# A planner's assumed DMA rate, lowered from 295 to 280 for the last token group of a decoder block

## The chip, the cores and the metric

The kernel runs on one core of one Trainium2 chip, as one program. The metric is the device time of that program in microseconds (us); of several runs the median counts. Engines are called by the profile's names: PE is TensorE, PEld its weight loads, DVE is VectorE, ACT is ScalarE, POOL is GpSimd and SP is SyncE.

## What is computed

One layer of a decoder block on 1024 tokens with 1024 channels, all in float32. Three token mixers (stick-breaking attention, dilated window attention, attention into 256 memory tokens) run on one normalised input, are gated and summed, and go through an output projection. Then comes an expert layer, which is what the change is about:

```python
s1, i1 = lax.top_k(sc[:, :, 0], 16); s2, i2 = lax.top_k(sc[:, :, 1], 16)
...
top_s, pos = lax.top_k(cand, PEER_TOPK)
idx = jnp.take_along_axis(cand_idx, pos, axis=-1)
gate = jax.nn.softmax(top_s, axis=-1)
...
act = gelu(einsum('chkd,cd->chk', u[ic], hc)); w = gc * act
return einsum('chk,chkd->cd', w, v[ic])
```

Each token has 8 heads, and each head picks 16 of 16384 experts. An expert is a row of 1024 numbers in a table `u` and one in a table `v`. A token's 128 chosen rows of `u` are multiplied with the token, and the 128 rows of `v` are summed with the weights that come out.

## The kernel before, in words

The 1024 tokens are 8 tiles of 128. They go through the mixers in three groups, `GROUPS = (2, 3, 3)`: group 0 holds tiles 0 and 1, group 1 tiles 2 to 4, group 2 tiles 5 to 7. `phase1` (one call for each group) runs these stages in order: stick-breaking, dilated and memory attention, gating (weights `w_gate` and `w_o`), the output projection (`out_proj`, weights `w_out`), the norm (`ffn_norm`) and the experts' query projection and choice (`select`, weights `w_pq`; the rest of the choice is `topk`, run in small pieces beside other work by `sides`).

The expert layer is done in two ways. Tiles 4 and 6 (`DENSE`) are done densely: all 16384 experts are multiplied, in the generator `dense`, which begins when the last group has ended and `stored` holds both tiles. The six other tiles are done by gathers (`Experts`). A gather step (`Experts.step`) handles one choice for each of 128 rows: POOL issues an indirect DMA of 128 rows of `u` and one of 128 rows of `v` (L1097, 0.5 MB each), DVE multiplies the `u` rows with the tokens' rows `hb` and sums (L1151), ACT and DVE make a weight, and PE adds the weighted `v` rows into `po` (L1177). PE and ACT also spread the tokens' rows into `hb` (L1090, L128). A tile has 128 steps, so there are 768 steps in all. `u` blocks are fetched 5 steps ahead, `v` blocks have 6 buffers (`UP, VP = 5, 6`).

A tile can be gathered once `topk` has put its row numbers, `iT`, and its weights, `gT`, (L1011 and L1013) into the list `ready`. Tiles 0 and 1 become ready when group 0 ends and are gathered while group 1 is computed; tiles 2 and 3 beside group 2; tiles 5 and 7 beside the dense part.

What is issued between two gather steps is set by a planner at the end of `block_kernel`. It keeps two running sums, `pe` and `dma`, in planned ns. A piece of the main work (`fill`, one `yield` of `rest()`, which chains the three groups and `dense`) adds its matmul cost times `slow` to `pe`, and its bytes divided by the rate `bw[0]` to `dma`. A gather step adds `TOKEN_NS` = 700 to `pe`, and `TOKEN_BYTES / bw[0]` to `dma`:

```python
            while filler[0] is not None and (dma > pe or pe < due):
                a, b = fill(1)
                pe += a
                dma += b
            pe += TOKEN_NS
            dma += TOKEN_BYTES / bw[0]
            if ex.step():
```

So a smaller rate makes a gather step look longer, and more main work is issued between two steps. The rate is `BW[0]` = 295 (bytes per ns) for the three groups, and `rest()` sets it to `BW[1]` = 360 when the groups are over (L1405). `TOKEN_BYTES` is 1,073,152, so that a step counts 3638 ns at 295. When the main work is used up, the remaining steps are issued one after the other. The planner's sums only set an order; they are not times of the chip. A scheduler then puts each engine's queue in order.

Of the kernel before, what the change touches and what calls it, by code (L numbers as in the profile page):

```python
# [34 lines left out]
RUN = 22  # L35


BW = 295.0, 360.0
SLOW = 1.38, 1.1
TOKEN_NS, TOKEN_BYTES = 700.0, 128 * 8192 + 3 * 8192.0  # L40
LEAST = 3000.0
# [36 lines left out]
def block_kernel(ctx: ExitStack, tc: tile.TileContext, io):  # L78
# [109 lines left out]
    def gap_tables():  # L188
        d32 = tmp.tile([128, 32], F32, name="on")
        nc.vector.tensor_scalar(d32, iota[:, :32], 4.0, rows[:, 1:2], op0=OP.mult, op1=OP.subtract)  # L190
        for (dil, nb), o, w, num in zip(DIL, gofs, gwid, gnum):
            diff = dmat if dil == 1 else d32
            for bd in range(num):
                c = o + (num - 1 - bd) * w
                t = gaps[:, c:c + w]
                bad = tmp.tile([128, 128], F32, name="on")[:, :w]
                b2 = tmp.tile([128, 128], F32, name="onm")[:, :w]
                nc.vector.tensor_scalar(t, diff, -1.0, 128.0 * bd, op0=OP.mult, op1=OP.add)
                nc.vector.tensor_scalar(bad, t, 0.0, HUGE, op0=OP.is_lt, op1=OP.mult)
                nc.vector.tensor_scalar(b2, t, float(128 * dil), HUGE, op0=OP.is_gt, op1=OP.mult)  # L200
                nc.vector.tensor_max(bad, bad, b2)
                if dil > 4:
                    gi = small.tile([128, 32], I32, name="gi")
                    nc.vector.tensor_copy(gi, t)
                    nc.vector.tensor_scalar(gi, gi, dil - 1, None, op0=OP.bitwise_and)
                    nc.vector.tensor_scalar(b2, gi, 0.0, HUGE, op0=OP.not_equal, op1=OP.mult)
                    nc.vector.tensor_max(bad, bad, b2)
                nc.vector.tensor_max(t, t, bad)
# [36 lines left out]
    def load(out, src):  # L245
        count(out)
        nc.sync.dma_start(out, src)
# [81 lines left out]
    def norm_T(xT, n, gain, out):  # L329

        p = bank()
        for k in range(KD):
            sq = tmp.tile([128, NMAX], F32, name="sq")
            actf(sq[:, :n], xT[:, k, :n], AF.Square)
            mm(p[:, :n], ones, sq[:, :n], start=k == 0, stop=k == KD - 1)
        yield
        y = rstd_rows(p[:, :n], n, D)
        for k in range(KD):
            nc.vector.scalar_tensor_tensor(out[:, k, :n], xT[:, k, :n], gain[:, k:k + 1], y[:, :n],
                                           op0=OP.mult, op1=OP.mult)  # L340
        yield
# [23 lines left out]
    def both(gidx, h, n):  # L365

        if gidx not in SPLIT:
            return h, None
        parts = []
        for k in range(0, KD, 4):  # L370
            parts.append(tuple(x.rearrange("p (k n) -> p k n", k=4) for x in spare()))
            halves(*(x[:, :, :n] for x in parts[-1]), (h[0] if type(h) is list else h)[:, k:k + 4, :n])
        return h, parts
# [21 lines left out]
    def memory_kv(pipe, weights, mh):  # L395
        kv = big.tile([128, 2048], F32, name="big")
        kTm = kv[:, :1024].rearrange("p (h m) -> p h m", h=4)
        vm = kv[:, 1024:].rearrange("p (m c) -> p m c", m=2)
        for h in range(4):
            p = proj_T(weights("w_kv", h), mh, MEM)  # L400

            def done(y, p=p, h=h):
                nc.vector.scalar_tensor_tensor(kTm[:, h, :], p[:, :MEM], gk_mem, y[:, :MEM],
                                               op0=OP.mult, op1=OP.mult)
            part = head_norm(p, MEM, 128, ones, done)
            pipe.tick()
            pipe.push(part)
            yield
        for h in range(4):
            proj_v(weights("w_kv", 4 + h), mh, 2, vm[:, :, h * 128:(h + 1) * 128], 0)  # L410
            pipe.tick()
            yield
        nc.scalar.dma_start(c_mem, kv)

    def subs(G):

        return [(i, min(SUB, G - i)) for i in range(0, G, SUB)]

    def stick_breaking(pipe, weights, hT, n0, G, oT):
        N = G * 128  # L420
        t0 = n0 * 128
        for p in range(4):
            kv = big.tile([128, 2048], F32, name="big")
            kT = kv[:, :1024]
            v = kv[:, 1024:].rearrange("p (t c) -> p t c", t=NT)
            if n0:
                load(kT[:, :t0], c_sbk[p, :, :t0])
                load(v[:, :n0], c_sbv[p, :, :n0])
            q = qpad[:, 2 * (p % 3):2 * (p % 3) + 2]
            pq = proj_T(weights("w_in", p), hT, N)  # L430
            for s in range(2):
                r = slice(64 * s, 64 * s + 64)
                nc.vector.tensor_scalar(q[r, s, :N], pq[r, :N], 0.125, None, op0=OP.mult)
            pipe.tick()
            yield
            pk = proj_T(weights("w_in", 4 + p), hT, N)
            actf(kT[:, t0:t0 + N], pk[:, :N], AF.Copy)
            pipe.tick()
            yield
            proj_v(weights("w_in", 8 + p), hT, G, v, n0)  # L440
            if n0 + G < NT:
                nc.scalar.dma_start(c_sbk[p, :, t0:t0 + N], kT[:, t0:t0 + N])
                nc.scalar.dma_start(c_sbv[p, :, n0:n0 + G], v[:, n0:n0 + G])
            pipe.tick()
            yield
            for i, g in subs(G):
                args = pipe, kT, v, q[:, :, i * 128:(i + g) * 128], n0 + i, oT[:, p, i * 128:(i + g) * 128]
                yield from stick_single(*args) if g == 1 else stick_part(*args[:5], g, args[5])
# [568 lines left out]
    def phase1(gidx, n0, G, out):  # L1017
        N = G * 128
        pipe = Pipe()
        weights = Weights(gidx)  # L1020
        hT = wide.tile([128, 8, NMAX], F32, name="wide")
        load(hT[:, :, :N], io["xT"][:, :, n0 * 128:n0 * 128 + N])
        norm = norm_T(hT, N, g_mix, hT)
        if gidx == 0:
            memT = big.tile([128, 8, MEM], F32, name="big")
            load(memT, io["memT"])
            mh = big.tile([128, 8, MEM], F32, name="big")
            yield from norm_T(memT, MEM, g_mem, mh)
            kv = memory_kv(pipe, weights, both(gidx, mh, MEM))
            next(kv)  # L1030
            next(norm)
            yield next(kv)
            next(norm)
            yield next(kv)
            yield next(kv)
            hT = both(gidx, hT, N)
            yield from kv
            weights.ahead = AHEAD
            gap_tables()
        else:  # L1040
            yield from norm
            hT = both(gidx, hT, N)
        oT = act.tile([128, 10, NMAX], F32, name="oT")
        yield from stick_breaking(pipe, weights, hT, n0, G, oT)
        mem = memory_attn(pipe, weights, hT, n0, G, oT)
        yield from dilated(pipe, weights, hT, n0, G, oT, mem)
        yield from mem
        mT = wide.tile([128, 8, NMAX], F32, name="wide")
        pipe.flush()
        yield from gating(pipe, weights, hT, N, oT, mT)  # L1050
        x2 = wide.tile([128, GMAX, D], F32, name="wide")
        yield from out_proj(weights, mT, n0, G, x2)
        h2T = [big.tile([128, 8, NS], F32, name="big") for _ in subs(G)]
        yield from ffn_norm(x2, n0, G, h2T)
        yield from select(pipe, weights, (h2T, None), n0, G, out)
# [332 lines left out]
    def rest():  # L1388
        n0 = built = 0
        odd = False  # L1390
        for g in range(len(GROUPS)):
            for stage in phase1(g, n0, GROUPS[g], ready):
                if stage and built < ND:

                    want = sum(n < n0 for n in DENSE)
                    while len(stored) < want:
                        sides(1)
                    odd = not odd
                    for _ in range(999 if stage == 2 else 1 + odd):
                        if built < want:  # L1400
                            built = next(gates)
                yield
            n0 += GROUPS[g]
        front.close()
        slow[0], bw[0] = SLOW[1], BW[1]  # L1405
        yield from dense()

    filler = [rest()]
    slow, bw = [SLOW[0]], [BW[0]]
    pe = dma = due = 0.0  # L1410
# [86 lines left out]
```

## Time and profile before

| | us |
|---|---|
| median of 3 runs (3557.21 to 3573.94) | 3561.07 |
| the profiled execution's own time | 3568.14 |
| its span, first to last instruction | 3566.4 |
| first gather step's DVE instruction | 494.9 |
| group 2 begins (first PE work of its stick-breaking stage) | about 1366 |
| group 2 has ended (505 steps gathered) | about 2377 |
| the dense products begin in earnest | about 2650 |
| main work ended, gathers alone from here | about 3396 |

How to read it: the busy tenths cut the span into 40 slices of 89 us. A table of windows gives, for each stretch of the span, every engine's busy time with its number of instructions in brackets, the granted TensorE clock, the mean busy share of the 16 DMA engines and the rate. A line of waits says who waited for whom, how long in total, how often, and how long at most. The chain of waits is followed back from the last instruction: at each moment it names the one thing that the end was waiting for. A matmul in float32 shows as two records; so a gather step has 8 records of L1177.

### The profile page before, as it was taken

The page shows a single profiled execution, that of the slowest core. Times are in us where ns is not written, and L with a number is a line of the kernel's source. Part 1 is how long each engine was busy: PE and PEld are TensorE (multiplying, and loading weights), DVE is VectorE, ACT ScalarE, POOL GpSimd, SP SyncE. Part 2 cuts the span into 40 slices and gives each one's busy share as a digit, 9 for nine tenths or more (in the row PEclk, how much of TensorE's full clock was granted, in tenths as well). Part 3 has the DMA queues.
Part 4 walks back from the last instruction along what each step waited for, and adds up shares of the span by engine and source line. Part 5 has one row for each costly group of instructions (what it writes and reads, how often), then busy time and mean ns, then how long its engine had stood idle before and what let it go on. Part 6 is the DMA issues. An engine that isn't in the chain of part 4 may idle for free.

```text
span 3566.4 us, 60764 instructions
## 1 busy us (share of the span) xinstructions
PE 3196.1 (90%) x22802; PEld 2361.1 (66%) x22802; DVE 2341.1 (66%) x5985; ACT 1353.6 (38%) x2729; POOL 1778.4 (50%) x1544
## 2 busy tenths in 40 slices
PE   6999989989999889999998999776779999999954
PEld 6889856656555766666565657654568888888710
DVE  5444487565545468996656665798867677777654
ACT  4443135554411214656544222222324444444410
POOL 0000036656566556666555655566745444544476
PEclk9989989999999999999999999897899999999965
DMA  4425669999899999999998999989999999999999
GB/s 151 139 84 182 206 221 334 333 348 331 313 406 392 403 363 347 337 331 350 331 355 296 391 391 400 350 325 348 393 386 393 365 382 384 394 379 372 344 383 362
DMA packets 346430, 1185.54 MB, mean 332 GB/s; under 512 B 38744, under 2 KB 80216, under 8 KB 326680
## 3 DMA queue, kind: packets, MB, share of 16 engines
q0 software_dynamic: 221184, 805.40, 59.6%
q1 hardware_dynamic: 102672, 337.95, 26.0%
q10 hardware_dynamic: 22280, 38.31, 2.8%
q8 instruction: 180, 2.95, 0.3%
q14 instruction: 114, 0.93, 0.1%
HBM read 1142.18 MB, written 39.32 MB: 331 GB/s over the span
## 4 chain that ended last, share of the span: by engine, by line
PE 61%; DMA 15%; DVE 13%; issue 5%; ACT 3%; POOL 2%; ACTq 0%; SPq 0%; POOLq 0%; DVEq 0%
PE bank L117 32%; PE bank L1195 20%; PE po L1177 7%; DMA u<-in_u,iT 7%; DVE u L1151 3%; DMA v<-in_v,iT 3%; PE pb L1090 1%; DMA b3d<-sp 1%; PE bank L121 1%; POOL v L1097 1%; POOL u L1097 1%; DMA g<-gd 1%; ACT L126 1%; DMA gd<-g 1%; ACT e L128 1%
## 5 line engine op out<-in xcount | busy, mean ns | idle before, releaser
L1097 POOL DMA_INDIRECT u<-in_u,iT x768 | 916.2, 1193 | 956.1 <-DVE i L865 489.6
L1097 POOL DMA_INDIRECT v<-in_v,iT x768 | 861.4, 1122 | 818.8 <-PE po L1177 646.0
L1151 DVE SCALAR_TENSOR_TENSOR u<-u,hb 128x1024 f32<-128x1024 f32 x768 | 926.7, 1222 | 440.1 <-ACT hb L128 256.3
L1177 PE MATMUL po<-v,wz 128*32 128x256 f32 x6144 | 444.8, 416 | 155.3 <-DMA v<-in_v,iT 88.6
L117 PE MATMUL bank<-wide,w 128*128 128x384 f32 x1536 | 519.6, 492 | 1.8 <-DMA w<-in_w_gate 1.8
L1177 PEld LDWEIGHTS po<-v,wz 128*32 128x32 f32 x6144 | 182.0, 115 | 375.0 <-DMA v<-in_v,iT 119.0
L117 PEld LDWEIGHTS bank<-wide,w 128*128 128x128 f32 x1536 | 292.3, 192 | 201.3 <-issue 6.8
L128 ACT ACTIVATE hb<-pb 128x512 f32<-128x512 f32 x384 | 208.2, 594 | 397.2 <-PE pb L1090 251.3
L117 PEld LDWEIGHTS bank<-w,wide 128*128 128x128 f32 x2304 | 263.0, 192 | 7.4 <-issue 2.2
L117 PE MATMUL bank<-w,wide 128*128 128x128 f32 x2304 | 265.3, 275 | 0.2 <-DMA w<-in_w_out 0.2
L1195 PE MATMUL bank<-hh,ul 128*128 128x256 f32 x848 | 240.0, 283 | 1.2 <-DVE ul L1275 1.2
L1195 PE MATMUL bank<-hh,uh 128*128 128x256 f32 x848 | 240.9, 284 | 0.0
L1195 PE MATMUL bank<-hl,uh 128*128 128x256 f32 x848 | 239.9, 283 | 0.0
L117 PE MATMUL bank<-big,w 128*128 128x256 f32 (+1 forms) x1280 | 235.6, 341 | 1.2 <-DMA w<-in_w_pq 1.2
L117 PEld LDWEIGHTS bank<-big,w 128*128 128x128 f32 x1280 | 208.3, 193 | 27.0 <-issue 3.0
L128 ACT ACTIVATE e<-bank 128x512 f32<-128x512 f32 (+2 forms) x208 | 109.6, 527 | 306.8 <-PE bank L117 301.2
L1195 PE MATMUL bank<-vh,wh 128*128 128x512 f32 x512 | 202.9, 403 | 3.1 <-ACT vh L128 3.1
L1195 PE MATMUL bank<-vl,wh 128*128 128x512 f32 x512 | 201.9, 394 | 2.1 <-DVE vl L1275 2.0
L1195 PE MATMUL bank<-vh,wl 128*128 128x512 f32 x512 | 199.4, 389 | 0.0
L126 ACT ACT_TABLE_LOAD x144 | 184.8, 1283 | 21.7 <-issue 8.8
L128 ACT ACTIVATE w<-bank 128x256 f32<-128x256 f32 x128 | 49.3, 385 | 366.9 <-PE bank L1195 285.5
L1275 DVE TENSOR_TENSOR vl<-vr,vh 128x1024 fp32r<-128x1024 f32 x128 | 156.9, 1226 | 32.7 <-ACT vh L128 32.7
(297 smaller groups left out, 5659.9 us busy)
## 6 DMA issues: line engine op xcount, KB each, us to landing
ur<-in_uT SPq DMA_DIRECT2D x64, 1024.0 KB
vr<-in_vd SPq DMA_DIRECT2D x64, 1024.0 KB
w<-in_w_in SPq DMA_DIRECT2D x102, 512.0 KB
w<-in_w_gate SPq DMA_DIRECT2D x72, 512.0 KB
w<-in_w_pq SPq DMA_DIRECT2D x48, 512.0 KB
g<-gd SPq DMA_DIRECT2D x16, 1024.0 KB
w<-in_w_o SPq DMA_DIRECT2D x48, 256.0 KB
w<-in_w_out SPq DMA_DIRECT2D x24, 512.0 KB
```

Of the source, the lines that this page charges most:

```text
L117: nc.tensor.matmul(out, lhsT, rhs, **kw)
L121: nc.tensor.transpose(out, in_, ident)
L126: nc.scalar.preload_act_table_set(s)
L128: nc.scalar.activation(out, in_, f, **kw)
L1090: nc.tensor.matmul(pb, which[:, jj].rearrange("p q s -> p (q s)"), box["b3"][:, f], start=True, stop=True)
L1097: nc.gpsimd.indirect_dma_start(out=t, out_offset=None, in_=io[kind], in_offset=bass.IndirectOffsetOnAxis(ap=ap, axis=0))
L1151: nc.vector.scalar_tensor_tensor(u, u, 1.0, self.hb, op0=OP.mult, op1=OP.mult, accum_out=self.parts[:, i:i + 1])
L1177: nc.tensor.matmul(po[32 * k:32 * k + 32, h:h + 256], wz[:, i, :], v[:, 256 * k:256 * k + 256], start=jj == 0 and i == 0, stop=jj == QB - ...
L1195: nc.tensor.matmul(out, lhsT, rhs, **kw)
L1275: nc.vector.tensor_sub(lo, r[:, x], hi)
```

## The change

`BW` gets a third rate, 280, and at the start of each group the planner's rate is set: 295 for groups 0 and 1, 280 for group 2. In group 2 a gather step then counts 1,073,152 / 280 = 3833 ns instead of 3638. The bytes of the main work are divided by the same rate. Nothing is computed otherwise, and the dense part keeps 360.

```diff
-BW = 295.0, 360.0
+BW = 295.0, 360.0, 280.0
...
         for g in range(len(GROUPS)):
+            bw[0] = BW[0] if g < 2 else BW[2]
             for stage in phase1(g, n0, GROUPS[g], ready):
```

Followed through the program, the planner's sums place these numbers of gather steps beside the stages of group 2 (before, after): stick-breaking 81, 75; dilated and memory attention 64, 59; gating 69, 64; `out_proj` 13, 11; `ffn_norm` 3, 3; `select` 37, 35. Group 2 ends after step 505 before and after step 485 now, of the 512 steps that tiles 0 to 3 have. From there to the last dense product the planner places 203 steps before and 202 now.

The first place in the orders is POOL's queue at the end of group 2; a row is an indirect DMA of a gather step, and ` x6` stands for six in a row. Before, the rows are the `u` blocks from the 509th and the `v` blocks from the 505th on; the 513th `u` block is the first of tile 5:

```order
L1097 DMA u<-in_u,iT 128x1024
L1097 DMA v<-in_v,iT 128x1024
L1097 DMA u<-in_u,iT 128x1024
L1097 DMA v<-in_v,iT 128x1024
L1097 DMA u<-in_u,iT 128x1024 x2
L1097 DMA v<-in_v,iT 128x1024 x6
L1097 DMA u<-in_u,iT 128x1024 x5
L1097 DMA v<-in_v,iT 128x1024
L1097 DMA u<-in_u,iT 128x1024
```

After, at the same two `u` blocks (the 512th and the 513th, in the middle of these rows):

```order
L1097 DMA v<-in_v,iT 128x1024
L1097 DMA u<-in_u,iT 128x1024
L1097 DMA v<-in_v,iT 128x1024
L1097 DMA u<-in_u,iT 128x1024
L1097 DMA v<-in_v,iT 128x1024
L1097 DMA u<-in_u,iT 128x1024
L1097 DMA v<-in_v,iT 128x1024
L1097 DMA u<-in_u,iT 128x1024
L1097 DMA v<-in_v,iT 128x1024
```

Before, the six last `v` blocks of tile 3 stand together, with no `u` block between them, and five `u` blocks of tile 5 follow at once; after, `u` and `v` blocks alternate across the same border.

The second place is DVE's queue where `topk` writes tile 5's row numbers and weights (L1011, L1013); a row of L1151 is a gather step. Before (the row of L1151 is step 512, the last of tile 3):

```order
L963 CAST wide<-ab 128x128
L965 CAST wide<-ab 128x128
L964 TENSOR_SCALAR ab<-ab 128x128
L966 SCALAR_TENSOR_TENSOR wide<-wide 128x128
L1151 SCALAR_TENSOR_TENSOR u,parts<-u,hb 128x1024
L1011 CAST iT<-bank 128x4x32
L1013 COPY gT<-bank 128x4x32
```

After (the first row of L1151 is step 491):

```order
L963 CAST wide<-ab 128x128 x2
L964 TENSOR_SCALAR ab<-ab 128x128 x2
L965 CAST wide<-ab 128x128
L1151 SCALAR_TENSOR_TENSOR u,parts<-u,hb 128x1024
L1011 CAST iT<-bank 128x4x32
L1013 COPY gT<-bank 128x4x32
L966 SCALAR_TENSOR_TENSOR wide<-wide 128x128
```

So tile 5's numbers are written 21 steps earlier in the count of gather steps, with 21 steps of tile 3 still to be done.

The third place is DVE's queue where the dense part ends: `vl` (L1275) is the last split of dense weights, and `ur` (L1373) adds the dense sums to the residual stream. Before, where the last row of L1151 ahead of L1373 is step 708:

```order
L1151 SCALAR_TENSOR_TENSOR u,parts<-u,hb 128x1024
L1275 TENSOR_TENSOR vl<-vr,vh 128x1024
L1165 TENSOR_TENSOR gel<-gel,gT 128x4
L1346 TENSOR_TENSOR wl<-w,wh 128x256
L1166 TENSOR_TENSOR wz<-gel,spread 128x128
L1151 SCALAR_TENSOR_TENSOR u,parts<-u,hb 128x1024
L1275 TENSOR_TENSOR vl<-vr,vh 128x1024
L1182 TENSOR_TENSOR row<-row,po 128x256
L1373 TENSOR_TENSOR ur<-ur,bank 128x512 x4
L1151 SCALAR_TENSOR_TENSOR u,parts<-u,hb 128x1024
```

After, where the last row of L1151 ahead of the first L1373 is step 688:

```order
L1275 TENSOR_TENSOR vl<-vr,vh 128x1024
L1346 TENSOR_TENSOR wl<-w,wh 128x256
L1165 TENSOR_TENSOR gel<-gel,gT 128x4
L1151 SCALAR_TENSOR_TENSOR u,parts<-u,hb 128x1024
L1275 TENSOR_TENSOR vl<-vr,vh 128x1024
L1166 TENSOR_TENSOR wz<-gel,spread 128x128
L1151 SCALAR_TENSOR_TENSOR u,parts<-u,hb 128x1024
L1373 TENSOR_TENSOR ur<-ur,bank 128x512 x2
L1151 SCALAR_TENSOR_TENSOR u,parts<-u,hb 128x1024
L1373 TENSOR_TENSOR ur<-ur,bank 128x512 x2
```

Behind the first of these additions 60 steps were left before (768 less 708), and 80 are left now.

## The prediction

> **What bounds the kernel now.** I began with the table of windows, cut at the stage borders of group 2 (loads of each stage's weights mark them) and of what follows. The columns are the window, its length, then busy time of PE, PEld, DVE, ACT and POOL, the granted clock, the DMA share and GB/s.
>
> ```profile
> 1366.00:1610.00 244.00, 228.29 (x1646) 153.93 (x1647) 233.03 (x785) 141.88 (x230) 155.29 (x131) 0.97 0.91 330
> 1610.00:1850.00 240.00, 224.15 (x1709) 147.50 (x1711) 144.88 (x314) 131.10 (x236) 142.74 (x132) 0.96 0.93 344
> 1850.00:2155.00 305.00, 292.40 (x1899) 180.99 (x1891) 191.96 (x473) 99.17 (x264) 173.19 (x159) 0.98 0.96 360
> 2155.00:2225.00 70.00, 70.00 (x636) 59.81 (x638) 38.00 (x89) 13.37 (x41) 42.49 (x39) 1.00 1.03 409
> 2225.00:2377.00 152.00, 126.68 (x946) 102.78 (x939) 116.83 (x491) 39.34 (x109) 87.64 (x76) 0.91 0.94 355
> 2377.00:2450.00 73.00, 30.18 (x243) 18.44 (x242) 65.90 (x217) 15.46 (x37) 36.63 (x32) 0.63 0.80 292
> 2450.00:2650.00 200.00, 155.08 (x1023) 109.50 (x1023) 157.66 (x515) 55.09 (x179) 125.71 (x103) 0.91 1.00 386
> 2650.00:3396.00 746.00, 739.70 (x5276) 627.49 (x5271) 532.36 (x825) 346.13 (x573) 356.28 (x274) 1.00 0.98 376
> 3396.00:3555.00 159.00, 77.64 (x546) 18.42 (x545) 83.07 (x156) 17.79 (x45) 121.59 (x118) 0.55 1.01 394
> ```
>
> The first five rows are group 2, 1011 us long. PE is busy in 941.5 of them (93%), and the DMA engines' share is 0.91 to 1.03. Two resources are nearly full, and the question of this change is which of them a gather step really costs there. The last row is the tail: main work is over, PE is half idle, and gathers alone run at 394 GB/s.
>
> Second, who waits for whom in group 2. These are rows of the groups by line for 1366 to 2377 us, PE's and then POOL's: count, busy time and mean ns, idle time before them and its releasers.
>
> ```profile
> L1177 PE MATMUL po<-v,wz 128*32 128x256 f32 x2144 | 141.4, 393 | 35.1 <-DVE wz L1166 22.8 <-DMA v<-in_v,iT 10.2 <-issue 2.2
> L1090 PE MATMUL pb<-b,which 96*128 96x512 bf16 x132 | 41.9, 391 | 0.3
> L1097 POOL DMA_INDIRECT u<-in_u,iT x267 | 308.9, 1157 | 168.4 <-DVE u L1151 57.6 <-issue 46.0 <-DVE sc L982 9.0
> L1097 POOL DMA_INDIRECT v<-in_v,iT x268 | 294.2, 1098 | 241.5 <-PE po L1177 185.5 <-issue 39.5 <-PE bank L117 8.0
> ```
>
> PE waited 10.2 us for gathered `v` rows in 1011; POOL waited 185.5 us for PE to give back a `v` buffer, and 57.6 us for DVE to give back a `u` buffer. So for the most part the gathers wait for the compute engines, and not the other way round.
>
> Third, whether PE's busy time hides waiting. The same matmul of the output projection is in group 0, where no gathers run (first row, 345 to 380 us), and in group 2 (second row, 2155 to 2225 us, DMA share 1.03):
>
> ```profile
> L117 PE MATMUL bank<-w,wide 128*128 128x128 f32 x174 | 19.6, 275 | 0.0
> L117 PE MATMUL bank<-w,wide 128*128 128x128 f32 x384 | 44.0, 275 | 0.0
> ```
>
> 19.6 / 174 is 113 ns and 44.0 / 384 is 115 ns: full DMA engines slow this matmul by under 2%. PE's busy time is work.
>
> Fourth, the chain of waits for group 2, by line:
>
> ```profile
> by line: PE bank L117 46.3%; DMA u<-in_u,iT 10.1%; PE po L1177 8.5%; issue 4.9%; DVE u L1151 4.7%; DMA v<-in_v,iT 3.7%; DMA b3d<-sp 2.1%; PE bank L121 1.8%; PE pb L1090 1.6%; POOL v L1097 1.3%; POOL u L1097 1.2%; DMA w<-in_w_gate 1.1%; ACT
> ```
>
> PE's main work (L117) has the largest share, and everything that belongs to gather steps has 10.1 + 8.5 + 4.7 + 3.7 + 1.6 + 1.3 + 1.2 = 31.1%.
>
> **The change, part by part.** It adds and removes no work. It takes 20 gather steps out of group 2 (505 less 485) and, since the dense part keeps its rate and holds 203 or 202 steps either way, hands them on to the tail, which grows from 60 steps to 80. So there is a price at the end, a saving in group 2, and a smaller thing at the border between them.
>
> *The tail.* These are the 60 last steps' DVE instructions (durations, first and last start) and what DVE waited for ahead of them, from 3396 us on:
>
> ```profile
> L1151 DVE SCALAR_TENSOR_TENSOR u<-u,hb x60: 1211/1225/1287, 3401.7 to 3554.4; 128x1024 f32<-128x1024 f32 x60
> ...
>   DMA u<-in_u,iT: 65.1, 51
> ```
>
> (3554.4 - 3401.7) / 59 = 2.588 us for a step, and DVE waits for rows 51 times in 60, so the tail is bound by transfers. Nothing lies beside these steps that could hide more of them. 20 x 2.588 = **+51.8 us**. This term I hold for nearly certain; its bounds are 2.5 and 2.7 us for a step, 50 to 54. DMA: Bandwidth & Descriptors in the Trainium skill (section Bandwidth) gives the SBUF ports 435 GB/s; the 805.40 MB of the gathers' queue over 768 steps are 1.049 MB a step, which would be an estimated 2.41 us and 48.2 us for the term. The row shows 405 GB/s, and the row decides.
>
> ```profile
> q0 software_dynamic: 221184, 805.40, 59.6%
> ```
>
> *Group 2.* What a step is worth there no row says directly, so it is bounded. From below, only PE's own time for it goes: L1177 and L1090 together are 141.4 + 41.9 = 183.3 us for 268 steps (2144 / 8), or 0.68 us, and 20 of them are 13.7 us. From above, its transfers go in full, as in the tail: 51.8 us. Between them lies the chain: 31.1% of 1011 us is 314 us, or 1.173 us for each of 268 steps, and 20 x 1.173 = **-23.5 us**. I take this value, since it weighs PE-bound and transfer-bound moments by their share on the path. It is nearer to the lower end, as the releasers above are too. By stages it fits what each is full of: stick-breaking (6 fewer steps) has DVE busy for 233.0 of 244 us, with L1151's 1.22 us for a step; gating and the output projection (7 fewer) have PE busy for 362.4 of 375; the last stage (2 fewer), with PE at 126.7 of 152, may give back transfers in full.
>
> *The border.* At the end of group 2 the queue of before has no rows of tile 3 left to fetch ahead, and the next `u` blocks wait until tile 5's numbers are written. POOL's rows there, with start, duration and the idle time ahead:
>
> ```profile
> 2400.52 1.44 POOL L1097 DMA_INDIRECT v<-in_v,iT  x1 [0.30 <-issue]
> 2410.50 0.93 POOL L1097 DMA_INDIRECT u<-in_u,iT  x1 [8.54 <-DVE gT L1013]
> ```
>
> This wait of 8.54 us goes, since 21 steps of tile 3 are still to be done when `gT` is written. What is late next is DVE: from 2377 to 2450 us it is busy for 65.9 of 73 us with the choice for tiles 5 and 6, which no change of the order shortens, and the dense part can't begin ahead of tile 6. So the gathers gain a head start, and the path gains it only as far as the transfers bound the stretch from 2450 to 2650 (DMA share 1.00, but DVE 157.7 and PE 155.1 of 200). Bounds 0 and 8.5; I take half, **-4 us**. The dense part from 2650 to 3396 has PE busy for 739.7 of 746 us and keeps its steps: 0.
>
> *Sum.* 51.8 - 23.5 - 4 = +24.3 us. Against the profiled execution's 3568.14 that is 3592.4. That execution is 7.1 us above the median of the runs, 3561.07, so against the median it is 3585.4; I forecast **3585 us**, 0.7% slower. Half a per cent, 17.8 us, is about what a measurement of this kernel can tell from no change: "same" is 3543.3 to 3578.9.
>
> **The rivals.** *The transfers are the bound of group 2 as well.* Then a step saved there gives back its 2.59 us, the tail takes the same, and only the border is left: 0 to -8.5, so 3553 to 3561. For it speaks the DMA share of 0.91 to 1.03; against it, that POOL waits 185.5 us for PE's buffers while PE waits 10.2 us for `v`. Perfetto Trace Analysis in the Trainium skill (section Identifying the Most-Contended Engine) says that matmul busy time doesn't tell how near TensorE is to its limit, and that weight-load busy time does; PEld is busy for 645 of 1011 us, 64%, so that by this rule PE has room and this rival would hold. The 113 and 115 ns above speak against reading it so here. I give it 0.24.
>
> *PE alone is the bound of group 2.* Then the saving is its lower end and the border gives nothing: 51.8 - 13.7 = +38, 3599 us. For it speaks the gating stage (PE 292.4 of 305); against it 13.8% of the chain on gathered rows in flight. 0.16.
>
> *Faster: every idle moment of the DMA engines is lost time.* They would then be the bound from group 2 to the end, moved steps would cost nothing on balance, and the change would win what they stood idle for want of rows: 0.06 x 152 + 0.20 x 73 = 9.1 + 14.6 = 24 us, 3537 us. It takes over from "same" where a step in group 2 is worth at least 2.6 us and more than 18 of these 24 us fill. For it speaks the row of 0.80; against it that only one wait of 8.54 us in that stretch is for tile 5's numbers, and that DVE is the busy engine there. 0.08.
>
> **How the numbers follow.** My own case, a step worth about 0.8 to 1.8 us in group 2, spans +8 to +36 and has 0.52; 0.11 of that lies below +17.8. So slower by over 0.5% is 0.41 + 0.16 = 0.57, within 0.5% is 0.11 + 0.24 = 0.35, and faster is 0.08. The range runs from the transfers' case nearly in full, 3552, to just above PE's case, 3604; it leaves out the faster rival and the ends, less than 0.2. Cases of both signs don't hold most of the chance, but the likeliest one's own range is 3569 to 3597.
>
> **What the new profile would show.** The tail: about 80 instructions of L1151 behind the last dense split, near 2.59 us apart, and its length at 159 + 52, or 211 us. Group 2: 248 steps instead of 268, with a length of about 987 us; at 960 or less the transfers were the bound, at 997 or more PE alone. The border: no wait of POOL's `u` for `gT`, and the stretch to the dense products shorter by 0 to 8 us. The dense part: 746 us as before. The forecast is wrong if group 2 shrinks by more than 45 us, or if the dense part changes its length by more than 10 us, which no term above has; a queue order that a scheduler has made anew in group 2 could also stall PE or DVE in places that no row of before shows.

## The result, and the profile after

The changed kernel takes 3619.62 us (median of 6 runs, 3612.58 to 3631.05), the kernel before 3571.22 us beside it (6 runs, 3557.21 to 3574.48). The ratio is 1.0147, with a 95% interval of 1.012 to 1.0174: about 52 us slower (48 by the medians), where 24 were forecast, and above the forecast's range of 3552 to 3604. Some 10 us of the distance to 3585 are the reference: the forecast started from 3561.07 us, the median of three runs, and six give 3571.22. Its profiled execution took 3627.54 us, with a span of 3625.8.

These are the windows of the changed kernel, cut at the same places of the program as those of before (for the last two rows at the last dense sum; columns as before):

```profile
1364.00:1607.00 243.00, 227.18 (x1612) 154.70 (x1613) 228.11 (x775) 141.06 (x227) 143.87 (x125) 0.96 0.88 315
1607.00:1846.00 239.00, 225.56 (x1711) 152.75 (x1711) 140.06 (x302) 128.24 (x233) 130.30 (x121) 0.97 0.88 325
1846.00:2148.00 302.00, 289.03 (x1833) 178.38 (x1832) 182.22 (x459) 94.45 (x259) 163.90 (x148) 0.96 0.92 341
2148.00:2214.00 66.00, 65.94 (x589) 57.40 (x588) 33.04 (x76) 10.87 (x33) 35.24 (x32) 1.00 0.99 381
2214.00:2370.00 156.00, 130.94 (x940) 106.31 (x941) 117.19 (x509) 39.25 (x111) 82.80 (x74) 0.91 0.91 334
2370.00:2443.00 73.00, 26.40 (x205) 14.85 (x205) 64.08 (x205) 13.70 (x29) 35.56 (x30) 0.63 0.80 285
2443.00:2644.00 201.00, 158.94 (x1019) 113.37 (x1017) 153.22 (x493) 55.32 (x184) 112.56 (x99) 0.89 0.97 373
2644.00:3407.00 763.00, 751.55 (x5332) 636.07 (x5332) 537.87 (x838) 347.57 (x577) 361.80 (x278) 0.99 0.97 371
3407.00:3614.00 207.00, 100.74 (x672) 20.16 (x670) 107.26 (x203) 22.70 (x57) 157.37 (x157) 0.53 1.02 401
```

Group 2 (five rows) lasts 1006 us, where it was 1011 and should have been 987. It has 20 steps less, and its DMA share fell in every row, so the transfers made room; the time hardly moved. The border (sixth row) still lasts 73 us. The tail has 80 steps, by the row of L1151 in it:

```profile
L1151 DVE SCALAR_TENSOR_TENSOR u<-u,hb x80: 1211/1226/1260, 3406.6 to 3613.7; 128x1024 f32<-128x1024 f32 x80
```

From first to last they take 207.1 us, 2.62 us for a step, against 152.7 us before: +54.4. The first of them starts at 3406.6, where it was 3401.7: all that lies ahead of the tail has become 4.9 us longer with 20 steps fewer in it. Group 2 gave 5 and the start of the program 2, the dense part took 11 (762.6 us from 2644 to the first tail step, 751.7 before), and the stretch between took 1.

Who waits for whom in group 2 (1364 to 2370 us), PE's rows and POOL's:

```profile
L1177 PE MATMUL po<-v,wz 128*32 128x256 f32 x1984 | 134.9, 405 | 24.9 <-DVE wz L1166 20.3 <-DMA v<-in_v,iT 3.6 <-issue 1.1
L1090 PE MATMUL pb<-b,which 96*128 96x512 bf16 x122 | 39.1, 391 | 0.6 <-ACT hb L128 0.5
L1097 POOL DMA_INDIRECT v<-in_v,iT x249 | 271.5, 1090 | 285.5 <-PE po L1177 239.4 <-issue 33.9 <-PE bank L117 5.8
```

PE's work for the steps fell by 6.5 + 2.8 = 9.3 us and its wait for `v` rows by 6.6, yet POOL waits even longer for PE's buffers (239.4 us, 185.5 before). These 16 us of room on PE didn't shorten the group. This is the changed kernel's chain of waits for it, to be read beside the one in the prediction:

```profile
by line: PE bank L117 58.4%; PE po L1177 10.0%; DVE u L1151 4.3%; DMA u<-in_u,iT 3.7%; issue 2.1%; PE pb L1090 2.0%; DMA c_dvc<-sp 1.9%; DMA b3d<-sp 1.5%; PE bank L121 1.4%; DMA v<-in_v,iT 1.4%; DVE sc L866 0.7%; DMA w<-in_w_in 0.6%; ACT L1
```

Gathered rows in flight (`u` and `v`) fell from 13.8% of the chain to 5.1%, and PE's main work (L117) rose from 46.3% to 58.4%. The steps that left took waits for rows off the path, and the path runs through PE's work instead.

### The profile page after: what moved, and what is told of

Its sections match the earlier page's. It is cut to its first block, busy times and chain, and to the rows that moved or that the text cites. A ratio compares the mean times of both kernels' runs of the same rounds, so it can differ in the third digit from the quotient of the medians.

```text
span 3625.8 us, 60784 instructions
## 1 busy us (share of the span) xinstructions
PE 3221.2 (89%) x22802; PEld 2373.2 (65%) x22802; DVE 2340.7 (65%) x5985; ACT 1347.1 (37%) x2725; POOL 1757.0 (48%) x1544
## 4 chain that ended last, share of the span: by engine, by line
PE 63%; DVE 13%; DMA 13%; issue 5%; ACT 4%; POOL 2%; ACTq 1%; SPq 0%; POOLq 0%; DVEq 0%
PE bank L117 34%; PE bank L1195 20%; PE po L1177 7%; DMA u<-in_u,iT 4%; DVE u L1151 4%; DMA v<-in_v,iT 2%; PE pb L1090 1%; DMA gd<-g 1%; PE bank L121 1%; DMA b3d<-sp 1%; POOL u L1097 1%; DMA vr<-in_vd 1%; ACT L126 1%; POOL v L1097 1%; DMA g<-gd 1%
## 5 line engine op out<-in xcount | busy, mean ns | idle before, releaser
L1097 POOL DMA_INDIRECT v<-in_v,iT x768 | 840.7, 1095 | 893.9 <-PE po L1177 724.0
L1151 DVE SCALAR_TENSOR_TENSOR u<-u,hb 128x1024 f32<-128x1024 f32 x768 | 924.6, 1223 | 450.9 <-ACT hb L128 285.8
L1177 PE MATMUL po<-v,wz 128*32 128x256 f32 x6144 | 461.0, 428 | 183.4 <-DMA v<-in_v,iT 100.5
L117 PE MATMUL bank<-wide,w 128*128 128x384 f32 x1536 | 520.7, 493 | 0.0
L117 PEld LDWEIGHTS bank<-wide,w 128*128 128x128 f32 x1536 | 293.5, 193 | 198.3 <-issue 8.5
L117 PEld LDWEIGHTS bank<-w,wide 128*128 128x128 f32 x2304 | 262.9, 192 | 7.7 <-issue 2.3
L117 PE MATMUL bank<-w,wide 128*128 128x128 f32 x2304 | 265.4, 276 | 0.2
L117 PE MATMUL bank<-big,w 128*128 128x256 f32 (+1 forms) x1280 | 236.3, 343 | 1.0 <-DMA w<-in_w_pq 1.0
L117 PEld LDWEIGHTS bank<-big,w 128*128 128x128 f32 x1280 | 209.4, 194 | 27.1 <-issue 2.5
L1275 DVE TENSOR_TENSOR vl<-vr,vh 128x1024 fp32r<-128x1024 f32 x128 | 157.0, 1226 | 35.0 <-ACT vh L128 35.0
```

The source lines that it names most:

```text
L117: nc.tensor.matmul(out, lhsT, rhs, **kw)
L1097: nc.gpsimd.indirect_dma_start(out=t, out_offset=None, in_=io[kind], in_offset=bass.IndirectOffsetOnAxis(ap=ap, axis=0))
L1151: nc.vector.scalar_tensor_tensor(u, u, 1.0, self.hb, op0=OP.mult, op1=OP.mult, accum_out=self.parts[:, i:i + 1])
L1177: nc.tensor.matmul(po[32 * k:32 * k + 32, h:h + 256], wz[:, i, :], v[:, 256 * k:256 * k + 256], start=jj == 0 and i == 0, stop=jj == QB - ...
L1275: nc.vector.tensor_sub(lo, r[:, x], hi)
```

## The experiments

In all of them a "step" is a gather step, and each ratio is against the kernel before on the same chip. "Group 2 with border" is the time from the first weight load of group 2 to the load of the dense tokens: 1087.1 us before, 1083.4 after.

**What a step is worth in group 2.** The first theory (the "hidden theory" below) was that 280 shows the true price: a step there runs in waits of the main work and is worth 0.2 us. The rival was that the forecast's 1.17 us is right and the queue order of the changed kernel lost some 19 us. A rate of 265 moves 40 steps instead of 20:

```diff
-BW = 295.0, 360.0, 280.0
+BW = 295.0, 360.0, 265.0
```

> Group 2 planned at 265: 465 steps by its end instead of 505, 41 more in the tail. Hidden theory (a gather step in group 2 runs in waits of the main work and is worth about 0.2 us at the margin, as the 20 steps of the change gave back 4 us): group 2 shorter by 8 us, tail longer by 41 x 2.59 = 106 us, in all about +98 us, ratio 1.027. Rival (a step is worth the 1.17 us of the chain of waits, and the changed kernel lost 19 us by an unlucky queue order): group 2 shorter by 47 us, in all +59 us, ratio 1.016.

It took 3649.47 us, a ratio of 1.0221 (1.0196 to 1.0245), or 79 us: between the two. In its profile group 2 with border came down to 1042.5 us, by 44.6, or 1.11 us for each of 40 steps. So in this order a step does have about the price of the chain, and the theory of free steps fell. The total is worse than that price because another stretch grew: from the load of the dense tokens to the last dense sum it took 990 us, where it was 973, with as many steps in it. The second run moves 21 steps, as the change does, but all of them out of the attention stages:

```diff
-            bw[0] = BW[0] if g < 2 else BW[2]
+            seen = False
             for stage in phase1(g, n0, GROUPS[g], ready):
+                seen = seen or stage is not None
+                bw[0] = BW[2] if g == 2 and not seen else BW[0]   # BW[2] = 265
```

> The rate is 265 in the attention stages of group 2 alone and 295 from gating on: 484 steps by the end of the group, as many as in the changed kernel, but all 21 taken out ahead of gating. Hidden theory: the attention stages are full of waits between ACT, DVE and PE, the steps ran in these, and the stages get shorter by under 5 us; tail +54, in all +50, ratio 1.014. Rival, chain price: the stages get shorter by 25 us, in all +29, ratio 1.008.

The ratio is 1.0144 (1.0125 to 1.0162), as the first theory wanted, but for another reason: the attention stages did become 22.3 us shorter (507.6 to 485.3), 1.1 us a step. The last stage of the group, `select`, with nearly the same steps, took 190.4 us where it took 175.2, and the border 86.4 instead of 82.0. So a later stage with no change of rate lost part of what the first ones gave back, and group 2 with border is 12 us shorter in all (1075.0). Part of the loss may be chance: `select` took 176.8 and 183.7 us in two executions of the changed kernel.

The change does away with a wait of POOL for tile 5's numbers. A rate of 310 makes this wait longer instead:

> Group 2 planned at 310: all 512 steps of tiles 0 to 3 are done shortly before it ends, and none is left at the border; the tail has 58 steps instead of 60. Hidden theory: 7 more steps in group 2 cost 1 to 2 us, the tail gives back 5, and up to 9 us of waiting for tile 5's numbers may come on top: ratio 0.998 to 1.002. Rival: 7 steps cost 8 us, the tail gives back 5: ratio 1.001 to 1.003. If rows left at the border are worth more than I think, the end of group 2 to the dense products gets longer by over 10 us.

The ratio is 1.0116 (1.0089 to 1.0143), worse than both theories had it. Its profile has the long wait, in POOL's waits and in the window of the border:

```profile
POOL u L1097 <- DVE gT L1013: 59.3, 1, 59.3
```

```profile
2384.00:2455.00 71.00, 33.95 (x274) 26.94 (x272) 61.51 (x259) 14.36 (x35) 17.32 (x12) 0.73 0.26 84
```

POOL stands still for 59.3 us, and the DMA engines are at 0.26. But this isn't where the profile lost its 28 us. The border lasts 71 us, where it lasted 82, and the stretch behind it 230, where it was 222. It is the stages ahead of the border that took 40 us more, with 16 more steps in them by the rows of L1151: 518, 335 and 192 us, where they were 508, 322 and 175. That is twice the price of the chain for 16 steps, and why it is so much isn't shown.

**Which engine a step costs.** Four kernels take one part of the steps of tiles 2 and 3 away, about 249 of the 268 in group 2, at the rates of before. Each ran once.

```diff
-                    v = self.vs.pop(0)
+                    v = self.vs.pop(0)
+                    if n in (2, 3):
+                        return
```

> The kernel before, with the matmuls of v rows (L1177) and the sum of them left out for tiles 2 and 3: the same gathers, DVE and ACT work, but about 249 steps of group 2 without their 0.53 us of PE. If PE is the bound of group 2 throughout: shorter by 130 us. Hidden theory: shorter by less than 40 us, as PE's work for the steps stood in its waits for others. If transfers are the bound: no shorter at all.

```diff
+            w = 512 if n in (2, 3) else D
-            ...indirect_dma_start(out=t, ..., in_=io[kind], ...)
+            ...indirect_dma_start(out=t[:, :w], ..., in_=io[kind] if w == D else
+                                        io[kind].rearrange("e (h d) -> (e h) d", h=2), ...)
```

> The kernel before, with half rows (2 KB instead of 4 KB, of other table rows) gathered for tiles 2 and 3, and the same instructions on PE, DVE, ACT and POOL: about 131 MB less to move in group 2. If transfers bound group 2: shorter by 50 us or more, until PE's 942 us stop it. Hidden theory and PE-bound theory: shorter by under 15 us.

```diff
+            f = slice(0, 64 if n in (2, 3) else D)
-            nc.vector.scalar_tensor_tensor(u, u, 1.0, self.hb, ...)
+            nc.vector.scalar_tensor_tensor(u[:, f], u[:, f], 1.0, self.hb[:, f], ...)
```

> The kernel before, with the DVE product of a gather step (L1151) cut to 64 of 1024 columns for tiles 2 and 3: about 249 steps of group 2 with 0.1 us of DVE instead of 1.22. If DVE is what a step costs: shorter by 100 us or more. Hidden theory: 10 to 30 us, in the stick-breaking stage, where DVE is busy for 233 of 244 us; nothing in gating.

```diff
-            out.append((n0 + i, iT, gT))
+            if n0 + i not in (2, 3):
+                out.append((n0 + i, iT, gT))
```

> The kernel before, with tiles 2 and 3 never gathered (their outputs are left out): group 2 has 18 steps instead of 268. Hidden theory at the margin's 0.2 us: group 2 is shorter by 50 us of 1011. Chain price of 1.17 us: shorter by 290 us. PE's price of 0.68 us: shorter by 170 us. An average far above the margin's price would say that only the last steps are free.

| group 2 with border | us | against 1087.1 |
|---|---|---|
| no matmuls of `v` rows | 1021.5 | -65.6 |
| half rows | 1065.5 | -21.6 |
| short DVE product | 1064.0 | -23.1 |
| no steps of tiles 2 and 3 | 952.1 | -135.0 |

The half rows settle the transfers. (In that kernel DVE multiplies `hb` with itself, and PE reads each half row twice, so that their work stays as it was.) Here are the gating windows of the kernel before and of the one with half rows:

```profile
1849.00:2171.00 322.00, 309.40 (x2024) 191.37 (x2023) 203.17 (x501) 105.19 (x281) 184.37 (x170) 0.98 0.96 362
```

```profile
1838.00:2157.00 319.00, 308.50 (x2025) 191.05 (x2024) 202.73 (x501) 104.91 (x280) 189.71 (x171) 0.98 0.71 227
```

The DMA share falls from 0.96 to 0.71 and the stage by 3 us, and all of group 2 with border by 21.6 us for half the bytes of 249 steps: the transfers were not its bound, and that rival is out. PE isn't the bound throughout either: half rows and the short DVE product leave PE's work as it was and still give back 21.6 and 23.1 us. How much of PE's work is on the path these runs don't say. 132 us less of it gave 65.6, but without this work the DMA share in gating rose to 1.01, so the transfers may have taken over there.

On the average of 250 steps the 135.0 us are 0.54 us a step, half of what the 40 steps at 265 gave. That would fit a group in which the first steps fill waits and the last ones stand on the path, but no run here shows it step by step.

**Is it 280, or the order?** The three kernels that changed an order lost some 20 us against their count of steps (280, 265 and 265 in the attention stages alone). So I left rate and number of steps alone and shifted where the steps fall: once, as group 2 begins, the planner is given 500,000 bytes (1.7 planned us at 295 and 1.8 at 280, half a step) or 1300 ns of PE cost (1.8 planned us).

```diff
+            if g == 2:
+                moved[0] += 500000.0      # or: cost[0] += 1300.0
             for stage in phase1(g, n0, GROUPS[g], ready):
```

> The changed kernel once more, for a second profile. If the lost time in group 2 comes from the order of its queues, the stages repeat within 1 or 2 us (attention stages 506.6 us, half-clock 34 us). If it is chance of one execution, the attention stages come out nearer to 499, as the line through 310, 295 and 265 has it.

> The changed kernel with 500,000 bytes added to the planner's count once, at the start of group 2: the same rate and 484 steps instead of 485 by its end, but each gather step stands at other pieces of the main work. Order theory (a step is worth 1.1 us, and where the steps fall moves group 2 by 10 us or more): group 2 differs from the changed kernel's by over 6 us, and on the line of the other rates it is 20 us shorter; ratio to before 1.008 to 1.012. Rival (280 has its price by the number of steps alone): within 3 us of the changed kernel, ratio 1.0147.

> The changed kernel with 1300 ns of PE cost added once at the start of group 2, a shift the other way: 485 steps by its end. Order theory: another group 2 time again, over 6 us from the changed kernel or from the run with added bytes, ratio to before between 1.007 and 1.018. Rival: within 3 us of the changed kernel, ratio 1.0147.

> The kernel before with the same 500,000 bytes added at the start of group 2: 505 steps by its end as before. Order theory: if before's order is a lucky one, group 2 gets longer by 5 to 20 us, ratio 1.002 to 1.006; if it is an average one, 0.997 to 1.003. Rival: ratio 1.000, group 2 within 3 us.

The second execution of the changed kernel repeats group 2 with border (1084.0 us) though not each stage (503.8 us for the attention stages, 506.6 in the first; 183.7 us for `select`, 176.8 in the first): some us wander from one execution to the next. The shifted kernels at 280 have 1073.7 and 1082.3 us there, and ratios of 1.014 (1.0115 to 1.0166) and 1.0141 (1.0115 to 1.0167), so the time at 280 is the same in three orders, and the expectation that it would scatter fell, though group 2 with border moved by 10 us in one of them. The surprise is the shifted kernel before: 3593.42 us, a ratio of 1.0072 (1.0047 to 1.0096), some 25 us for nothing but half a step's shift. Either before has a lucky order or its neighbour an unlucky one. Two more shifts of before and two rates between were to tell:

> The kernel before with 1300 ns of PE cost added once at the start of group 2: 506 steps by its end. If before's order is a lucky one: slower again, ratio 1.004 to 1.010. If the other shift was the unlucky one: ratio 0.998 to 1.002.

> The kernel before with 1,000,000 bytes added once at the start of group 2, twice the first shift: 504 steps by its end. Lucky order: ratio 1.004 to 1.010. Unlucky shift: 0.998 to 1.002.

> Group 2 planned at 290: 498 steps by its end, 7 fewer than before, and 67 left for the tail. By the number of steps at my prices (2.59 in the tail, 1.17 in group 2) it costs 10 us against before, ratio 1.003. If before's order is worth some 20 us by luck, it costs 30, ratio 1.008, at once with the first steps moved.

> Group 2 planned at 285: 492 steps by its end, 13 fewer than before, 74 left for the tail. By the number of steps alone it costs 18 us against before, ratio 1.005; with the loss of a lucky order 38 to 43, ratio 1.011 to 1.012.

And then, since these split, one more shift of each (1,000,000 bytes at 280, 2600 ns at 295). These two ran on a chip where the kernel before took 3714.64 us, so that only their ratios are used:

> The changed kernel with 1,000,000 bytes added once at the start of group 2: 484 steps by its end. If 280 has a good phase as 295 has: near 3595 us, ratio 1.006 to 1.009. If the steps themselves cost 38 us or more: 3606 to 3622 us, ratio 1.011 to 1.015.

> The kernel before with 2600 ns of PE cost added once at the start of group 2: 507 steps by its end. Two levels: within 4 us of 3569 or of 3594. A spread without levels: anywhere from 3560 to 3600.

| kernel | steps by the end of group 2 | ratio to before (95% interval) | group 2 with border, us |
|---|---|---|---|
| before, at 295 | 505 | 1 | 1087.1 |
| shifted by 1300 ns | 506 | 1.0009 (0.9996 to 1.0022) | 1095.2 |
| shifted by 500,000 bytes | 505 | 1.0072 (1.0047 to 1.0096) | 1095.4 |
| shifted by 1,000,000 bytes | 504 | 1.0079 (1.0062 to 1.0095) | 1097.1 |
| shifted by 2600 ns | 507 | 1.0061 (1.0033 to 1.0090) | other chip |
| rate 290 | 498 | 1.0027 (1.0016 to 1.0039) | 1073.8 |
| rate 285 | 492 | 1.0069 (1.0052 to 1.0086) | 1055.9 |
| rate 280, the change | 485 | 1.0147 (1.0120 to 1.0174) | 1083.4 |
| 280, shifted by 1300 ns | 485 | 1.0141 (1.0115 to 1.0167) | 1082.3 |
| 280, shifted by 500,000 bytes | 484 | 1.0140 (1.0115 to 1.0166) | 1073.7 |
| 280, shifted by 1,000,000 bytes | 484 | 1.0111 (1.0065 to 1.0157) | other chip |

At 295 five orders run from 1 to 1.0079, with a mean of 1.0044; before is the lowest. At 280 four run from 1.0111 to 1.0147, with a mean of 1.0135. The difference of the means, 0.0091 or 32 us, is an estimate of the price of the 20 steps; by the scatter of so few orders it is good to some 15 us either way. 0.0044 or 16 us more is how far the kernel before lies below the mean of its own setting. 290 and 285 came out close to their count of steps alone (10 and 18 us expected, 10 and 25 measured), not to the count with the lost luck: orders near before's level exist there too. 280's four orders found none.

The last column, from one profile each, shows where an order counts. 285 keeps 7 steps more in group 2 than 280 does, and yet is 27 us shorter there. (Its total doesn't show that in full: 13 more steps than before in the tail, and 12 us more between the border and the dense products, weigh against it.) These are group 2's windows from its first weight load to its last one, for before, 280, 285 and 265:

```profile
1341.00:2346.00 1005.00, 936.64 (x6780) 641.32 (x6780) 715.92 (x2082) 424.58 (x881) 598.59 (x533) 0.96 0.95 353
```

```profile
1339.00:2337.00 998.00, 930.69 (x6609) 642.69 (x6609) 690.67 (x2045) 413.67 (x862) 554.00 (x493) 0.96 0.91 334
```

```profile
1343.00:2318.00 975.00, 920.96 (x6677) 634.57 (x6677) 697.12 (x2058) 411.99 (x866) 562.64 (x504) 0.97 0.94 348
```

```profile
1340.00:2301.00 961.00, 906.15 (x6472) 629.39 (x6474) 662.67 (x1973) 404.51 (x847) 512.27 (x452) 0.97 0.89 324
```

Length less busy time, PE is idle for 68, 67, 54 and 55 us. So 280 took steps out of the group and left PE idle for as long as before, while 285 and 265 took some 13 us of its idle time out as well. Set against before's profile, a step is worth 0.2 us by the order of 280, 1.1 by that of 265 and 2.4 by that of 285: one order doesn't tell the price, even with some 0.5 us off for what a profile can wander.

What makes an order good is not shown. One trait goes with it, the granted clock. The spans and mean granted clocks of before, of the shift by 1300 ns, of the one by 500,000 bytes and of the one by 1,000,000 are:

```profile
core 0: 3566.4 us, clock 0.937
```

```profile
core 0: 3578.8 us, clock 0.937
```

```profile
core 0: 3587.1 us, clock 0.933
```

```profile
core 0: 3599.5 us, clock 0.931
```

In the traces' records the granted clock is 1 or one half, so (1 - clock) x 2 x span is the time at half clock: 449, 451, 481 and 497 us. The two slow orders have 30 to 48 us more of it in these executions. Over all runs they have 22 and 28 us more than the kernel before beside them, and half of that, 11 and 14 us, is lost where PE has work; the mean times differ by 24 and 29. So the clock goes together with about half of the difference. No run held the clock and changed the order, and it is not shown as the cause.

**The other way.** The dense part at 380 takes 26 steps out of the tail, where the change put 20 more:

```diff
-BW = 295.0, 360.0
+BW = 295.0, 380.0
```

> The kernel before, with the dense part planned at 380 instead of 360: 26 steps go from the tail into the dense part, the opposite of what the change does. If PE alone bounds the dense part, they cost 26 x 0.68 = 18 us there and give back 67 us in the tail: ratio 0.986. If its transfers bind as well (DMA share 0.98 at 376 GB/s), they cost 67 us there and the ratio is 1.000.

3554.85 us, a ratio of 0.9955 (0.9938 to 0.9973): between the two expectations, and faster than both kernels. Its windows from the load of the dense tokens to the first products, and on to the last dense sum:

```profile
2436.00:2683.00 247.00, 179.66 (x1119) 121.99 (x1119) 183.56 (x594) 61.78 (x199) 138.60 (x124) 0.85 0.98 379
2683.00:3459.00 776.00, 763.03 (x5472) 641.28 (x5476) 555.00 (x876) 352.40 (x589) 404.08 (x314) 0.99 1.00 389
```

They were 222 and 751 us, so 26 steps cost 50 us there, 1.9 each. In the tail they cost 2.6. On PE, DVE and POOL this kernel's queues are those of before, row for row, until the border, and group 2 with border took 1094.6 us where it took 1087.1: a single profile's difference of under 8 us says nothing here.

## Why the prediction was wrong

*The tail, +51.8.* Right: a step took 2.62 us, inside its bounds, and the term came out at +54.4, just above its own of 50 to 54.

*Group 2, -23.5.* As a mean over orders the price may hold: 54.4 - 32 = 22 us for the 20 steps in nine orders, wherever they were saved, with the same 15 us of doubt. For this order it was wrong: in the changed kernel's own execution the group gave back 5 us, with PE idle for as long as before. The bounds of 13.7 and 51.8 were taken for ends of what the count can do, and they are not ends for one order.

*The border, -4.* Wrong. The wait for `gT` is gone, as forecast, and the border is as long as before, 73 us, with DVE busy for 64.1 of them. POOL now waits there for DVE and PE otherwise:

```profile
POOL u L1097 <- DVE sc L966: 6.8, 1, 6.8
POOL u L1097 <- DVE u L1151: 4.7, 2, 4.1
POOL v L1097 <- PE po L1177: 3.9, 3, 3.0
```

*The dense part, 0.* Its steps are as many, but it took 11 us more in this execution, over the 10 us that the prediction itself named as a sign of being wrong. It took 9 more in the first shifted kernel before, which moved no step into or out of it (760 against 751 us, at a clock of 0.99 where it was 1.00). So it needs no moved steps.

```profile
2650.00:3401.00 751.00, 744.70 (x5322) 630.83 (x5318) 535.17 (x829) 346.84 (x575) 360.35 (x277) 1.00 0.98 375
```

```profile
2661.00:3421.00 760.00, 749.50 (x5332) 635.54 (x5333) 534.99 (x832) 345.83 (x573) 357.07 (x275) 0.99 0.97 370
```

The five profiles in which the clock never fell during the dense products (before, its shift by 1300 ns, 310, half rows, no steps of tiles 2 and 3) have 750 to 751 us there. The ten with 10 to 19 us at half clock and no steps added, the changed kernel's two among them, have 754 to 763; four with 3 to 7 us have 751 to 757. What set off these falls is open.

*The step that failed* is the group 2 term, -23.5, where the changed kernel gave back 5, and with it the zero for the dense part, where it took 11. Both fail in the same place: the sum was made "against the profiled execution's 3568.14" as if its order were any order with 505 steps, and the new one any order with 485. The last sentence of the prediction named a new order as a danger, but gave it no price and no chance. The runs give it one: at the same rate, of two shifts by half a step one costs this kernel 0.1% and the other 0.7%, as much as the 24 us forecast, a whole step costs 0.8%, and before stood at the good end. Of the some 50 us the steps are 32 (24 forecast) and the lost order about 16, by the estimate above. The range ended just above PE's case, +38, for want of this term; the reference, 10 us low, would not alone have put the time outside. Why one order leaves PE idle and another doesn't stays open.

*The rivals.* The transfers' case fell by the half rows. PE's case, whose +38 came nearest, is not settled: PE isn't the bound throughout, as the half rows and the short DVE product show, but an estimate of 32 us with 15 of doubt can't tell +38 from the forecast's +24. The rule of Perfetto Trace Analysis in the Trainium skill (section Identifying the Most-Contended Engine), that PE's busy time says little of its limit, would have favoured the transfers' case; the half rows (share 0.71, 3 us) speak against that reading here.

## What to carry to other kernels

What a step taken out of a full stage is worth came out near its share of the chain of waits only in the mean of several orders, far below its transfer time, and single orders lay anywhere from 0.2 to 2.4 us; where the step goes to a stretch with nothing to hide it, that stretch's row is the price, and here it held. When a planner or scheduler makes the order, compare a few shifted orders of each setting before crediting a setting with a difference under 1%: here five orders of one setting span 0.8%, and a forecast from one of them needs that span in its range.

## What the runs showed of the hardware

PE's granted clock is 1 or one half in the records of every profile here, and it drops in stretches of a few us after short waits, within group 2 as well. Here is a wait of PE for gathered rows in the kernel before, from the rows in order of time, and then two windows of 8 us behind it:

```profile
1378.45 1.08 PE L1177 MATMUL po<-v,wz 128*32 128x256 f32 x8 [4.95 <-DMA v<-in_v,iT]
```

```profile
1378.00:1386.00 8.00, 6.83 (x25) 3.07 (x26) 7.97 (x18) 0.28 (x1) 5.71 (x5) 0.57 1.03 409
1386.00:1394.00 8.00, 8.00 (x29) 4.82 (x28) 7.74 (x11) 0.16 (x1) 2.70 (x1) 1.00 0.67 241
```

The clock is 0.57 in the first window and 1.00 in the next, so a wait of 5 us costs some 3 us more behind it. TensorE: Matmul & The Clock Gate in the Trainium skill (section Part 1: The HAM clock gate) says that an idle window of about 3.4 us halves the clock and a busy one restores it; these rows agree. I had priced waits of PE at their length alone.
